# A two-layer decoder trunk on one core: where four table stores are queued, and where the side work stands in the first FFN

## The chip, the cores and the metric

The kernel runs on one core of a Trainium2 chip. The metric is the device time of one execution in microseconds (us). The core has five engines that are fed by queues of their own and run in the order of those queues: TensorE (PE, matmuls), VectorE (DVE), ScalarE (ACT), GpSimd (POOL) and SyncE (SP, which here only issues DMAs).

## The reference

`x` is 512 tokens by 1024 channels, `c` one conditioning vector. All is float32.

```python
c_act = jax.nn.silu(c)
for i in range(2):
    mod = c_act @ w_mod[i] + b_mod[i]
    sh1, sc1, g1, sh2, sc2, g2 = jnp.split(mod, 6, axis=-1)
    h = modulate(rms_norm(x, norm_mix[i]), sh1, sc1)
    y = (stick_breaking_attention, s5_ssm)[i](h, ...)
    x = x + g1[:, None, :] * y
    h = modulate(rms_norm(x, norm_ffn[i]), sh2, sc2)
    x = x + g2[:, None, :] * conv_ffn(h, w_up[i], conv_w[i], conv_b[i], w_down[i])
sh, sc = jnp.split(c_act @ w_fin + b_fin, 2, axis=-1)
return modulate(rms_norm(x, norm_out), sh, sc)

def conv_ffn(h, w_up, conv_w, conv_b, w_down):     # 1024 -> 2 x 2816 -> 1024
    up = causal_depthwise_conv(h @ w_up, width 3) + conv_b
    gate, val = jnp.split(up, 2, axis=-1)
    return (jax.nn.silu(gate) * val) @ w_down
```

The state-space layer `s5_ssm` needs tables that depend on the weights alone: powers of a complex decay, rotation angles, and products of them with its input and output matrices.

## The kernel before, in words

The stages follow each other: attention, first FFN, state-space layer, second FFN with the final norm. The activations lie with channels on the partitions and the 512 tokens along the free dimension. Each float32 matmul is made of three (`mm3`, lines 158, 161 and 162): weights and activations are split into a high part (ACT, line 152) and the rest (DVE, line 153), and high x high, low x high and high x low are summed in PSUM. Every weight tile is 128 x 1024, 512 KB, loaded by SP into one of three raw buffers (line 150) and then split into one of five pairs of buffers.

**First FFN.** The 22 blocks of 128 hidden channels are worked in groups of 8, 8 and 6 (`GROUPS`). A group has an up part, one *unit* per block: 48 matmuls of 128 x 512 for the gate half and the value half, then (`unit_out`) the convolution with three taps (ACT line 441, DVE line 443 twice per half), silu, product (line 453) and the split of the product into gH and gL (lines 457, 458). After the units comes the group's down part (`out_proj`): eight output tiles, each of 24 matmuls in the first two groups, each added to the residual x (line 334). Units 0 and 1 are computed together, ahead of the loop; so the loop starts with the third unit, `up0_2`. In a tile's name the first digit is the layer, the next the unit or group, the last the half or the output tile: `up0_9_1` is the value half of unit 9, `dn0_1_3` the fourth output tile of the second group.

Two kinds of side work are mixed in:

- *Gemvs.* The modulation vectors `mod` of the later layers are 72 products, each of a 128 x 1024 tile of `w_modT` with the broadcast `c_act`: a 512 KB load by SP (line 182, tiles `wg`, two buffers) and one multiply with a sum on DVE (line 183). `bg` (line 201) takes the next one from a list. In the first FFN one follows each output tile of the first two groups, and one follows a unit if the unit's place in its group is below a bound (line 504). The ACT and DVE work of units, weight splits and gemvs is held in program order by `follow`.
- *The preparation* of the state-space tables, `ssm_prep` (lines 828 to 1062), a generator that runs to its next `yield` at each call of `step`. `pace` (line 466) counts microseconds: each unit adds 11.0, each output tile 5.4, and each time 12.0 (`PACE`) are together, one step is taken. Steps 1 to 3 make powers of the decay (`pw`) and the factor `lf`; steps 4 to 8 build rotation tables `tb` in two halves on POOL by doubling (lines 833 to 838, 36 instructions each); step 5 has four transposes of `lf` on PE (line 933, into `ptl`), whose copy `lt` (ACT, line 935) is stored as `sL`. Each half of `tb` is stored by two DMAs to `sR` (line 955); there is one `tb` buffer. Then `b_re` and `b_im` are loaded into `ball` (line 969), POOL makes `bb` of them, and a loop of eight blocks follows, two steps each: POOL makes `bl` from loads `lam` and `bt` (lines 833 to 838) and `cl` from a load `bc` (lines 1036 to 1041), and one step later `direct` (line 976) multiplies `cl` by `bd` in 8 small matmuls on PE (line 980, into `pk0` to `pk7`): four of them need `cl` of line 1038, four that of line 1041. ACT and DVE make `kz` of the result (lines 982, 983), which goes to DRAM.

A scheduler that models time sets the order on each queue; the transposes of line 933 and the matmuls of line 980 are pinned to their place in the program on PE (`pe_pin`). In each queue, what stands behind a waiting instruction waits with it.

Of the kernel before, what the change touches and what calls it, by code (L numbers as in the profile page):

```python
# [41 lines left out]
PACE = 12.0  # L42
# [46 lines left out]
def _trunk(ctx, tc, I, out, tap):  # L89
    nc = tc.nc  # L90
    V, S, G, PE, SP = nc.vector, nc.scalar, nc.gpsimd, nc.tensor, nc.sync
# [13 lines left out]
    def bank(p=None, name="ps"):  # L105
        p = p or mm
        return p.tile([P, 512], F32, tag="b", name=name)
# [84 lines left out]
    def mcol(l, v, j):  # L192
        return l * 48 + v * 8 + j
# [211 lines left out]
    def ffn(l, R, prep=None, last=None, hook=lambda: None):  # L405
        b = mod[:, mcol(l, 3, 0):mcol(l, 3, 0) + KD]
# [3 lines left out]
        with ExitStack() as fc:  # L410
            fp = fc.enter_context(tc.tile_pool(name=f"ffn{l}", bufs=1, reuse_waits="tile"))

            def up_w(i, s):
                return load_w(up_src(l, i, s), name=f"up{l}_{i}_{s}"), bank(name=f"up{l}_{i}_{s}")
# [3 lines left out]
            i0 = 0  # L418
# [41 lines left out]

            i0 = 0
            step = None
            credit = [0.0]


            def pace(us):
# [6 lines left out]
            for gi, gn in enumerate(GROUPS):  # L473
                gs = []
                i = i0
                if gi == 2:
                    hook()
                if gi == 0:
                    if l:
                        hx, ws = pin["hw"]  # L480
                        hd = [(q, s, ws[2 * q + s], bank(name=f"up{l}_{q}_{s}")) for q in range(2) for s in range(2)]
                    else:
                        hx = None
                        hd = [(q, s) + up_w(q, s) for q in range(2) for s in range(2)]
                    head_mm(R, h, a, b, [q[2:] for q in hd])
                    if hx:
                        hx.close()
                    for q in range(4):
                        with behind_head(pin["head"][HEADW[q]]):
                            split_next(False)  # L490
                    pin["prep"] = [pin["split"]]
                    for q in range(2):
                        gs.append(unit_out(q, q, [hd[2 * q + s][3] for s in range(2)]))
                    i = 2
                    step = prep(fc) if prep else (lambda: None)
                for i in range(i, i0 + gn):
                    av = []
                    for s in range(2):
                        w, ps = take(), bank(name=f"up{l}_{i}_{s}")
                        for k in range(KD):  # L500
                            mm3(ps, wk(w, k), (h[0][k], h[1][k]), k == 0, k == KD - 1)
                        av.append(ps)
                    gs.append(unit_out(i, i - i0, av, split_next))
                    if l or i - i0 < (0, 3, 4)[gi]:
                        bg(BGU if l else 1, lined=True)
                    pace(11.0)

                def after():
                    if l == 0 and gi < 2:
                        bg(1, lined=True)  # L510
                    pace(5.4)

                head = None
                if gi == 2 and prep:
                    while step():
                        pass
                    head = [I["w_in"][bi * P:(bi + 1) * P, :] for bi in range(4)], "win"
                R2 = out_proj(lambda mt: I["w_down"][(l * KD + mt) * P:(l * KD + mt + 1) * P, i0 * P:(i0 + gn) * P], gs, mcol(l, 5, 0),
                         acc2 if gi == 2 else None, f"dn{l}_{gi}_", tail=TAIL + (FINT if last else 0), n=gn * P, after=after, last=last if gi == 2 else None, head=head,
                         getw=lambda mt: take(), step=split_next)  # L520
                i0 += gn
# [301 lines left out]
    sR = dram.tile([8, P, 2, 256], F32, tag="sR", name="sR")  # L823
# [4 lines left out]
    def ssm_prep(fc):  # L828
# [14 lines left out]
        def gen():  # L843
# [96 lines left out]
            for hb in range(2):  # L940
                ps_ = slice(hb * HP, (hb + 1) * HP)
                tb = pt_.tile([P, 2, HP, NC], F32, tag="tb", name="tb")
                tt = pt_.tile([P, 2, HP, 32], F32, tag="tt", name="tt")
                E.memset(tb[:, 0, :, 0:1], 1.0)
                E.memset(tb[:, 1, :, 0:1], 0.0)
                for q in range(6):
                    n = 1 << q
                    e0, e1 = bcast(co[:, 3 + q, ps_], n), bcast(si[:, 3 + q, ps_], n)
                    cmul(tb[:, 0, :, n:2 * n], tb[:, 1, :, n:2 * n], tb[:, 0, :, :n], tb[:, 1, :, :n], e0, e1, tt[:, 0, :, :n], tt[:, 1, :, :n])
                    if q > 3:  # L950
                        yield
                    if hb == 0 and q == 4:
                        lf_out()
                for ri in range(2):
                    SP.dma_start(sR[hb * 4:(hb + 1) * 4, :, ri, :].rearrange("b p n -> p b n"), tb[:, ri].rearrange("p (b q) c -> p b (q c)", b=4))
            tc1.close()

            tc2 = ExitStack()
# [342 lines left out]
    b = mod[:, mcol(2, 0, 0):mcol(2, 0, 0) + KD]  # L1301
# [154 lines left out]
```

## Time and profile before

| | |
|---|---|
| runs | 1210.58, 1212.62 and 1214.79 us, median 1212.62 |
| the profiled execution | 1211.41 us, its span (first to last instruction) 1209.4 us |
| PE busy | 1173.0 us, 97% of the span |
| DVE, ACT, POOL busy | 884.2, 563.8 and 264.0 us |
| mean granted TensorE clock | 0.989 of full speed |

A row of a timeline gives the start in us from the span's start, the duration in us, the engine, the line of the kernel, the operation, the tile written, the tiles read and, after x, how many like it were merged; in brackets stands how long the engine sat idle before it and what ended that. Matmuls overlap: the time from one start to the next, not the duration, is what one costs. SPq rows are DMAs being issued, not transferred. A row of a windows table gives the stretch and its length, then the busy time (and count) of PE, weight loads, DVE, ACT and POOL, the granted clock, and the DMA engines' busy share and GB/s.

### The profile page before, as it was taken

The numbers are of one execution on the slowest core, as the hardware profiler recorded it, in microseconds if no ns is written. First come the engines' busy times: TensorE is split into PE (matmuls) and PEld (weight loads), VectorE is DVE, ScalarE is ACT, GpSimd is POOL, SyncE is SP. The second block draws the span as 40 slices with busy tenths as digits, with TensorE's granted clock in tenths as the row PEclk, the third lists the DMA queues.
The fourth block names the chain that finished last, engine by engine and source line by source line (L and its number), as shares of the span: only waits on it lengthen the run. The fifth ranks groups of instructions, "written<-read, shape, count | busy, mean of one in ns | idle before, by whom it ended". The sixth has DMA issues, their size and how long they took to land.

```text
span 1209.4 us, 16352 instructions
## 1 busy us (share of the span) xinstructions
PE 1173.0 (97%) x6182; PEld 962.7 (80%) x6182; DVE 884.2 (73%) x1298; ACT 563.8 (47%) x886; POOL 264.0 (22%) x241
## 2 busy tenths in 40 slices
PE   8999999899999999989999999999999999999997
PEld 6877776588788787868888878789888888888887
DVE  6968888756896399997886679776598457744655
ACT  6756566346553133422444657744554234422443
POOL 1000000000098699989630000000000000000003
PEclk9999999899999999989999999999999999999999
DMA  8875555421234867878665599542257438532221
GB/s 306 319 242 174 192 175 190 157 88 53 73 119 131 239 235 225 252 229 291 217 184 152 188 292 342 186 159 68 70 175 236 130 106 208 157 110 82 79 79 70
DMA packets 93536, 210.99 MB, mean 174 GB/s; under 512 B 19601, under 2 KB 39953, under 8 KB 93458
## 3 DMA queue, kind: packets, MB, share of 16 engines
q1 hardware_dynamic: 85138, 207.86, 54.1%
q10 hardware_dynamic: 8320, 2.10, 0.8%
q8 instruction: 48, 0.79, 0.3%
q14 instruction: 30, 0.25, 0.1%
HBM read 188.68 MB, written 21.24 MB: 174 GB/s over the span
## 4 chain that ended last, share of the span: by engine, by line
PE 66%; DVE 12%; POOL 8%; DMA 6%; ACT 4%; issue 3%; SPq 2%; POOLq 0%; ACTq 0%; DVEq 0%
PE up L161 9%; PE up L162 9%; PE up L158 9%; PE dn L161 5%; PE dn L158 5%; PE dn L162 5%; PE o L756 1%; DMA bt<-in_b_imT_dram 1%; PE wo L158 1%; PE wos L158 1%; DVE ca L443 1%; PE wos L162 1%; PE wos L161 1%; PE wo L162 1%; PE wo L161 1%
## 5 line engine op out<-in xcount | busy, mean ns | idle before, releaser
L162 PE MATMUL up<-hH,up_l 128*128 128x512 f32 (+1 forms) x692 | 265.0, 385 | 4.9 <-DVE up_l L153 4.9
L161 PE MATMUL up<-hL,up_h 128*128 128x512 f32 (+1 forms) x692 | 264.9, 385 | 0.3 <-DVE hL L304 0.2
L158 PE MATMUL up<-hH,up_h 128*128 128x512 f32 (+1 forms) x692 | 261.3, 385 | 1.1 <-ACT hH L298 1.1
L443 DVE SCALAR_TENSOR_TENSOR ca<-up,small,ca 128x511 f32<-128x511 f32 (+1 forms) x176 | 131.4, 747 | 85.4 <-ACT ca L441 82.5
L183 DVE SCALAR_TENSOR_TENSOR wg<-wg,cact 128x1024 f32<-128x1024 f32 x96 | 125.1, 1318 | 42.4 <-DMA wg<-in_w_modT_dram 42.2
L162 PEld LDWEIGHTS up<-hH,up_l 128*128 128x128 f32 x692 | 130.5, 189 | 32.1 <-DVE up_l L153 6.8
L161 PEld LDWEIGHTS up<-hL,up_h 128*128 128x128 f32 x692 | 130.4, 189 | 26.4 <-DVE hL L304 0.9
L158 PEld LDWEIGHTS up<-hH,up_h 128*128 128x128 f32 x692 | 128.3, 188 | 27.9 <-ACT hH L298 1.5
L161 PE MATMUL dn<-gL,dn_h 128*128 128x512 f32 (+1 forms) x394 | 145.5, 369 | 2.7 <-DVE gL L458 2.7
L158 PE MATMUL dn<-gH,dn_h 128*128 128x512 f32 (+1 forms) x394 | 145.7, 371 | 0.5 <-ACT gH L457 0.5
L162 PE MATMUL dn<-gH,dn_l 128*128 128x512 f32 (+1 forms) x394 | 145.3, 369 | 0.0
L152 ACT ACTIVATE up_h<-up_r 128x1024 fp32r<-128x1024 f32 x84 | 88.3, 1053 | 107.6 <-DMA up_r<-in_w_up_dram 54.0
L153 DVE TENSOR_TENSOR up_l<-up_r,up_h 128x1024 fp32r<-128x1024 f32 x84 | 124.5, 1482 | 15.8 <-ACT up_h L152 14.9
L1328 POOL TENSOR_SCALAR xa<-x,Anorm_out 128x256 f32<-128x256 f32 x7 | 5.8, 828 | 576.3 <-ACT dn_h L152 561.5
L441 ACT ACTIVATE ca<-up,small 128x512 f32<-128x512 f32 x88 | 67.8, 771 | 102.4 <-PE up L162 102.4
L161 PEld LDWEIGHTS dn<-gL,dn_h 128*128 128x128 f32 x394 | 74.9, 190 | 15.3 <-DVE gL L458 3.0
L158 PEld LDWEIGHTS dn<-gH,dn_h 128*128 128x128 f32 x394 | 74.8, 190 | 13.7 <-ACT gH L457 0.9
L162 PEld LDWEIGHTS dn<-gH,dn_l 128*128 128x128 f32 x394 | 74.9, 190 | 12.2
L334 DVE SCALAR_TENSOR_TENSOR x<-dn,mod,x 128x512 f32<-128x512 f32 (+1 forms) x55 | 37.3, 679 | 61.1 <-PE dn L162 61.0
L450 ACT ACTIVATE ca<-ca 128x512 f32<-128x512 f32 x44 | 27.8, 633 | 90.1 <-DVE ca L443 88.4
L152 ACT ACTIVATE dn_h<-dn_r 128x1024 fp32r<-128x1024 f32 (+1 forms) x48 | 46.6, 981 | 49.8 <-PE dn L161 36.6
L153 DVE TENSOR_TENSOR dn_l<-dn_r,dn_h 128x1024 fp32r<-128x1024 f32 (+1 forms) x48 | 63.7, 1328 | 3.2 <-ACT dn_h L152 3.0
(304 smaller groups left out, 2258.8 us busy)
## 6 DMA issues: line engine op xcount, KB each, us to landing
wg<-in_w_modT_dram SPq DMA_DIRECT2D x96, 512.0 KB
up_r<-in_w_up_dram SPq DMA_DIRECT2D x84, 512.0 KB
dn_r<-in_w_down_dram SPq DMA_DIRECT2D x32, 512.0 KB
wgs<-in_w_modT_dram SPq DMA_DIRECT2D x16, 512.0 KB
dn_r<-in_w_down_dram SPq DMA_DIRECT2D x16, 384.0 KB
wv_r<-in_w_v_dram SPq DMA_DIRECT2D x8, 512.0 KB
wk_r<-in_w_qk_dram SPq DMA_DIRECT2D x8, 512.0 KB
wq_r<-in_w_qk_dram SPq DMA_DIRECT2D x8, 512.0 KB
```

The lines of the kernel that those rows point to most:

```text
L152: order("S", lambda: S.activation(wh[:, :n], raw[:, :n], AF.Copy))
L153: pin["split"] = order("V", lambda: V.tensor_tensor(wl[:, :n], raw[:, :n], wh[:, :n].bitcast(F32), ALU.subtract))
L158: ins = PE.matmul(ps, ah, bh, start=start, stop=False)
L161: PE.matmul(ps, ah, bl, start=False, stop=False)
L162: PE.matmul(ps, al, bh, start=False, stop=stop)
L183: mul = lambda: V.scalar_tensor_tensor(w, w, 1.0, cact, ALU.mult, ALU.mult, accum_out=raw[:, col:col + 1])
L334: add = lambda: V.scalar_tensor_tensor(xs, pv, gate, xs, ALU.mult, ALU.add)
L441: follow("S", lambda: S.activation(ca, ps, AF.Identity, bias=small[:, cb:cb + 1], scale=tapw[2]))
L443: follow("V", lambda: V.scalar_tensor_tensor(ca[:, q:], ps[:, :T - q], tapw[2 - q], ca[:, q:], ALU.mult, ALU.add))
L450: follow("S", lambda: S.activation(cg, cg, AF.Silu))
L756: ins = PE.matmul(po[pr][h2 * HD:(h2 + 1) * HD, j * P:], vn[:, j, hd:hd + HD], src, start=j == 0, stop=j == 3)
L1328: G.tensor_scalar(xa[k], x[k][:, cb], a[:, k:k + 1], 0.0, ALU.mult, ALU.add)
```

## The change

```diff
             i0 = 0
             step = None
-            credit = [0.0]
+            credit = [PACE]
...
                     gs.append(unit_out(i, i - i0, av, split_next))
-                    if l or i - i0 < (0, 3, 4)[gi]:
+                    if l or i - i0 < (6, 0, 3)[gi]:
                         bg(BGU if l else 1, lined=True)
                     pace(11.0)
...
                 for ri in range(2):
-                    SP.dma_start(sR[hb * 4:(hb + 1) * 4, :, ri, :].rearrange("b p n -> p b n"), tb[:, ri].rearrange("p (b q) c -> p b (q c)", b=4))
+                    G.dma_start(sR[hb * 4:(hb + 1) * 4, :, ri, :].rearrange("b p n -> p b n"), tb[:, ri].rearrange("p (b q) c -> p b (q c)", b=4))
```

The four stores of the rotation tables are issued by POOL instead of SP. Of the seven gemvs that follow units in the first FFN, four now follow units 2 to 5 of the first group (none before), none follow the second group's units (three before), and three follow the third group's (four before); since the list is taken in order, the 16 gemvs in the down parts are the next ones of the list, too. The pace starts with 12.0 to its credit, so each step of the preparation is called one unit, or about two output tiles, earlier; across the border of the first two groups the count falls so that step 11 (with `pk0`) comes two units earlier. The number of instructions of each kind stays.

**The transposes of `lf`.** They are pinned on PE, and now come one unit earlier. PE's queue before, at the end of the first group's up part:

```order
L161 MATMUL up0_7_1_3483<-hL7_2570,up0_7_1_h_3329 128x512
L162 MATMUL up0_7_1_3483<-hH7_2562,up0_7_1_l_3330 128x512
L933 MATMUL ptl_3535<-consts_87,lf_3338 128x128 x4
L158 MATMUL dn0_0_0_3549<-gH0_2887,dn0_0_0_h_3402 128x512
L161 MATMUL dn0_0_0_3549<-gL0_2888,dn0_0_0_h_3402 128x512
L162 MATMUL dn0_0_0_3549<-gH0_2887,dn0_0_0_l_3403 128x512
```

and in the changed kernel:

```order
L161 MATMUL up0_6_1_3419<-hL7_2570,up0_6_1_h_3259 128x512
L162 MATMUL up0_6_1_3419<-hH7_2562,up0_6_1_l_3260 128x512
L933 MATMUL ptl_3471<-consts_87,lf_3271 128x128 x4
L158 MATMUL up0_7_0_3485<-hH0_2555,up0_7_0_h_3335 128x512
L161 MATMUL up0_7_0_3485<-hL0_2563,up0_7_0_h_3335 128x512
L162 MATMUL up0_7_0_3485<-hH0_2555,up0_7_0_l_3336 128x512
```

They moved ahead of unit 7's 48 matmuls. They read `lf`, whose last instruction on POOL is that of line 838. POOL's queue before, around it (`tt` and `tb` are the rotation table's, 16x16 and 512 the two last doublings):

```order
L836 TENSOR_TENSOR lt1_3339<-pw_3063,fi_3066 128x256
L837 TENSOR_TENSOR lt2_3340<-pw_3063,fr_3065 128x256
L835 TENSOR_TENSOR tb_3424<-tt_3425 128x16x16
L838 TENSOR_TENSOR lf_3338<-lt1_3339,lt2_3340 128x8x32
L836 TENSOR_TENSOR tt_3425<-tb_3424,si_3195 128x16x16
L837 TENSOR_TENSOR tt_3425<-tb_3424,co_3194 128x16x16
L838 TENSOR_TENSOR tb_3424<-tt_3425 128x16x16
L833 TENSOR_TENSOR tt_3425<-tb_3424,co_3194 128x512
L834 TENSOR_TENSOR tt_3425<-tb_3424,si_3195 128x512
```

and in the changed kernel, with the first two of the four stores further down:

```order
L838 TENSOR_TENSOR tb_3360<-tt_3361 128x16x16
L836 TENSOR_TENSOR lt1_3272<-pw_2989,fi_2992 128x256
L837 TENSOR_TENSOR lt2_3273<-pw_2989,fr_2991 128x256
L833 TENSOR_TENSOR tt_3361<-tb_3360,co_3124 128x512
L834 TENSOR_TENSOR tt_3361<-tb_3360,si_3125 128x512
L838 TENSOR_TENSOR lf_3271<-lt1_3272,lt2_3273 128x8x32
L835 TENSOR_TENSOR tb_3360<-tt_3361 128x16x32
L836 TENSOR_TENSOR tt_3361<-tb_3360,si_3125 128x512
L837 TENSOR_TENSOR tt_3361<-tb_3360,co_3124 128x512
L955 DMA sR_113<-tb_3360 128x4x256
L838 TENSOR_TENSOR tb_3360<-tt_3361 128x16x32
L955 DMA sR_113<-tb_3360 128x4x256
```

Five instructions of the table that stood behind the last one of `lf` now stand ahead of it, while PE asks for `lf` one unit earlier.

**The first small matmuls, `pk0`.** PE's queue before has them behind unit 10:

```order
L161 MATMUL up0_10_1_4126<-hL7_2570,up0_10_1_h_3994 128x512
L162 MATMUL up0_10_1_4126<-hH7_2562,up0_10_1_l_3995 128x512
L980 MATMUL pk0_4188<-cl_3917,bd_3809 32x128 x8
L158 MATMUL up0_11_0_4216<-hH0_2555,up0_11_0_h_4075 128x512
L161 MATMUL up0_11_0_4216<-hL0_2563,up0_11_0_h_4075 128x512
L162 MATMUL up0_11_0_4216<-hH0_2555,up0_11_0_l_4076 128x512
```

and in the changed kernel behind unit 8, in two halves with three matmuls of unit 9 between:

```order
L161 MATMUL up0_8_1_3978<-hL7_2570,up0_8_1_h_3843 128x512
L162 MATMUL up0_8_1_3978<-hH7_2562,up0_8_1_l_3844 128x512
L980 MATMUL pk0_4037<-cl_3860,bd_3751 32x128 x4
L158 MATMUL up0_9_0_4065<-hH0_2555,up0_9_0_h_3895 128x512
L161 MATMUL up0_9_0_4065<-hL0_2563,up0_9_0_h_3895 128x512
L162 MATMUL up0_9_0_4065<-hH0_2555,up0_9_0_l_3896 128x512
L980 MATMUL pk0_4037<-cl_3860,bd_3751 32x128 x4
L158 MATMUL up0_9_0_4065<-hH1_2556,up0_9_0_h_3895 128x512
L161 MATMUL up0_9_0_4065<-hL1_2564,up0_9_0_h_3895 128x512
```

`pk0` moved two units ahead; `pk1` to `pk7` moved one unit (two output tiles in the down part) ahead.

**SP's queue between the groups.** Before, with what each issue waits for in brackets (DMAHW are earlier DMAs of SP, DMASW those of POOL):

```order
L150 DMA dn0_0_7_r_3716<-in_w_down_dram 128x1024 [waits DMAHW3_49,DVE_49]
L955 DMA sR_113<-tb_3622 128x4x256 [waits DMAHW0_49,Pool_49]
L955 DMA sR_113<-tb_3622 128x4x256 [waits Pool_49]
L182 DMA wg56_3688<-in_w_modT_dram 128x1024 [waits DMAHW2_49,DVE_49]
L150 DMA up0_8_0_r_3757<-in_w_up_dram 128x1024 [waits DMAHW4_49,DVE_49]
L969 DMA ball_3815<-in_b_re_dram 128x512 [waits DMAHW1_49,DMAHW0_49,PE_49]
```

and in the changed kernel:

```order
L150 DMA dn0_0_7_r_3734<-in_w_down_dram 128x1024 [waits DMAHW6_49,DVE_49]
L182 DMA wg60_3706<-in_w_modT_dram 128x1024 [waits DVE_49]
L150 DMA up0_8_0_r_3807<-in_w_up_dram 128x1024 [waits DMAHW7_49,DMAHW3_49,DVE_49]
L182 DMA wg61_3741<-in_w_modT_dram 128x1024 [waits DMAHW4_49,DVE_49]
L150 DMA up0_8_1_r_3842<-in_w_up_dram 128x1024 [waits DMAHW0_49,DVE_49]
L182 DMA wg62_3814<-in_w_modT_dram 128x1024 [waits DVE_49]
L150 DMA up0_9_0_r_3894<-in_w_up_dram 128x1024 [waits DMAHW1_49,DVE_49]
L969 DMA ball_3757<-in_b_re_dram 128x512 [waits DMASW1_49,DMASW2_49,DMASW0_49,DMASW3_49,PE_49,Pool_49]
```

The loads of unit 8's weights and of three gemvs no longer stand behind the stores; the load of `ball`, whose buffer is taken over from the tables, waits on SP for all four stores.

## The prediction

> **What bounds the kernel now.** I read the page's first part, then a table of stretches of 10 us over the first FFN, then the timelines of the engines there.
>
> ```profile
> PE 1173.0 (97%) x6182; PEld 962.7 (80%) x6182; DVE 884.2 (73%) x1298; ACT 563.8 (47%) x886; POOL 264.0 (22%) x241
> ```
>
> PE is the bound, so a change can only take away or add time in which PE waits, or in which its clock is lowered. All edits lie in the first FFN. The table (PE, weight loads, DVE, ACT, POOL, then the granted clock):
>
> ```profile
> 390.00:400.00 10.00, 10.00 (x46) 8.29 (x45) 0.00 (x0) 0.00 (x0) 9.12 (x11) 1.00 0.18 60
> ...
> 410.00:420.00 10.00, 7.78 (x29) 5.97 (x28) 5.32 (x5) 1.06 (x1) 6.83 (x7) 0.85 1.04 284
> ...
> 420.00:430.00 10.00, 10.00 (x44) 8.26 (x44) 10.00 (x11) 3.86 (x4) 9.68 (x7) 0.98 0.64 231
> ...
> 520.00:530.00 10.00, 7.13 (x30) 4.83 (x31) 10.00 (x8) 2.27 (x3) 7.20 (x6) 0.66 0.84 274
> ```
>
> From 390 to 400 us DVE and ACT do nothing at all; PE pays for it afterwards, at 410 to 420 and at 520 to 530, where it is idle and its clock falls. What PE waits for between 270 and 680 us (total, times, longest) and its timeline, with all its waits after 400 us in this FFN:
>
> ```profile
> PE up L162 <- DVE up_l L153: 4.9, 4, 2.2
> PE dn L161 <- DVE gL L458: 2.7, 1, 2.7
> ```
>
> ```profile
> 370.01 0.60 PE L933 MATMUL ptl<-consts,lf 128*128 128x128 f32 x4
> 370.36 0.47 PE L158 MATMUL dn<-gH,dn_h 128*128 128x512 f32 x1
> ...
> 413.99 0.39 PE L158 MATMUL up<-hH,up_h 128*128 128x512 f32 x1
> 414.22 0.39 PE L161 MATMUL up<-hL,up_h 128*128 128x512 f32 x1
> 416.82 0.61 PE L162 MATMUL up<-hH,up_l 128*128 128x512 f32 x1 [2.22 <-DVE up_l L153]
> 417.23 0.63 PE L158 MATMUL up<-hH,up_h 128*128 128x512 f32 x1
> ...
> 428.97 0.39 PE L158 MATMUL up<-hH,up_h 128*128 128x512 f32 x1
> ...
> 450.82 0.64 PE L980 MATMUL pk<-cl,bd 128*32 128x128 f32 x16
> ...
> 463.82 0.50 PE L162 MATMUL up<-hH,up_l 128*128 128x512 f32 x1 [0.79 <-DVE up_l L153]
> ...
> 476.89 0.50 PE L162 MATMUL up<-hH,up_l 128*128 128x512 f32 x1 [1.00 <-DVE up_l L153]
> ...
> 520.20 0.50 PE L158 MATMUL dn<-gH,dn_h 128*128 128x512 f32 x1 [0.46 <-ACT gH L457]
> 523.38 0.80 PE L161 MATMUL dn<-gL,dn_h 128*128 128x512 f32 x1 [2.67 <-DVE gL L458]
> ```
>
> The down part from 370.36 to 413.99 holds 192 matmuls, 0.227 us each; a unit of 48 takes 10.91. Unit 8 runs from 413.99 to 428.97, 14.98 us: 4.1 more than that, 2.4 of it the wait at 416.82 and 1.7 the half clock behind it (0.41 from 416.82 to 417.23). The four later waits sum to 4.9 idle, some 0.2 more each for restarting (0.50 instead of 0.39), and the clock of 0.66 means 6.8 us at half, of which some 3.2 fall on matmuls: 8.9 in all. The fourth wait of the first row, 0.89 at 327 us, lies ahead of all edits but a gemv and stays. So **13.0 us** is what the FFN could gain. The cause stands on SP and DVE:
>
> ```profile
> 374.44 4.85 SPq L150 DMA_DIRECT2D dn_r<-in_w_down_dram  x2
> 395.36 3.87 SPq L955 DMA_DIRECT2D sR<-tb  x2
> ...
> 402.81 0.33 SPq L969 DMA_DIRECT2D ball<-in_b_re_dram  x1
> ```
>
> ```profile
> 404.30 1.22 DVE L183 SCALAR_TENSOR_TENSOR wg<-wg,cact 128x1024 f32<-128x1024 f32 x1 [15.96 <-DMA wg<-in_w_modT_dram]
> ...
> 414.50 2.27 DVE L153 TENSOR_TENSOR up_l<-up_r,up_h 128x1024 fp32r<-128x1024 f32 x1
> ...
> 473.16 1.52 DVE L443 SCALAR_TENSOR_TENSOR ca<-up,small,ca 128x511 f32<-128x511 f32 x2
> ...
> 512.84 1.52 DVE L443 SCALAR_TENSOR_TENSOR ca<-up,small,ca 128x511 f32<-128x511 f32 x2
> ```
>
> SP issues nothing between 379.3 and 395.4: the second table's stores wait for POOL, and the loads of gemvs and of unit 8's weights stand behind them. DVE idles 15.96 us for a gemv's load, splits unit 8's weights late (414.50), and is behind PE until 523.
>
> **The stores and the loads that they held.** Off SP's queue, the stores no longer hold `wg` and `up0_8`; unit 8 starts without the wait: **-4.1**. SP now waits at `ball` instead, with `wg63` and `up0_9_1` behind. That is late by some 10 us for DVE, but `up0_9_1` is needed only when PE has done the first half of unit 9, after 440 (below). I cost it at nothing; with that cover gone it would be up to 6.
>
> **The gemvs.** One costs DVE 1.22 (row at 404.30) to, with POOL busy, 2.27 as the split of the same size. Four more in units 2 to 5 are 4.9 to 9.1 of DVE work, which delay splits; whatever PE loses by that before `pk0` is hidden by its wait there. In the second group, units without gemvs start their convolution at 473.16 (unit 11) and 512.84 (unit 15): 9.9 us each on DVE against 10.91 on PE. So once DVE is not behind, it stays so, and the later waits go: **-8.9**. In the third group PE never waits in this trace; one gemv less there is worth nothing.
>
> **The preparation.** Here PE starts to wait for POOL. POOL's timeline before:
>
> ```profile
> 357.49 0.74 POOL L838 TENSOR_TENSOR lf<-lt,lt 128x256 f32<-128x256 f32 x1
> 358.19 0.63 POOL L836 TENSOR_TENSOR tt<-tb,si 128x256 f32<-128x256 f32 x1
> ...
> 363.87 2.15 POOL L835 TENSOR_TENSOR tb<-tt 128x512 f32<-128x512 f32 x1
> ...
> 368.57 2.14 POOL L838 TENSOR_TENSOR tb<-tt 128x512 f32<-128x512 f32 x1
> 374.54 0.13 POOL L944 MEMSET tb<- 128x16 f32 x1 [3.83 <-DMA sR<-tb]
> ...
> 387.72 0.62 POOL L833 TENSOR_TENSOR tt<-tb,co 128x256 f32<-128x256 f32 x1
> ...
> 397.55 1.28 POOL L838 TENSOR_TENSOR tb<-tt 128x512 f32<-128x512 f32 x1
> ...
> 406.32 1.26 POOL L833 TENSOR_TENSOR t<-ball,fr 128x512 f32<-128x512 f32 x1 [6.80 <-DMA ball<-in_b_re_dram]
> ...
> 418.23 1.27 POOL L834 TENSOR_TENSOR t<-lam,bt 128x512 f32<-128x512 f32 x1 [2.54 <-DMA bt<-in_b_imT_dram]
> ...
> 435.11 2.29 POOL L1038 TENSOR_TENSOR cl<-t,t 128x576 f32<-128x576 f32 x1
> ...
> 440.41 1.43 POOL L1041 TENSOR_TENSOR cl<-t,t 128x576 f32<-128x576 f32 x1
> ...
> 462.69 2.37 POOL L1041 TENSOR_TENSOR cl<-t,t 128x576 f32<-128x576 f32 x1
> ```
>
> *Transposes.* PE gets there one unit earlier, at 370.01 - 10.91 = 359.1. The five table instructions now ahead of `lf`'s last took 358.19 to 363.87, 5.7; so `lf` is ready at 357.49 + 0.74 + 5.7 = 363.9. PE waits 4.8. A wait of 2.22 cost one stretch of half clock worth 1.7, the pair around 523 some 3.2; I take 2.5: **+7.3**. What else moves with the step waits too, and is covered: ACT's copy `lt` holds unit 6's silu, whose result PE needs only in the down part, after 376; the store `sL` on SP holds `dn0_0_3`, which DVE splits behind unit 7's work, after 376 as well. Unit 8 then ends at 413.99 + 10.91 + 7.3 = 432.2.
>
> *`pk0`* needs `cl`, which in this trace is ready at 440.41 + 1.43 = 441.84, 9 us before PE asks (450.82). Now PE asks at 432.2. When is `cl` ready? The first table still ends at 370.7. Issuing a store is not seen on POOL in this trace: between nothing (SP's issue of two took 3.87 with its waits) and one DVE instruction in the way (2.27) each; nearest is a small one, 0.5, with two ahead of the second table and two behind: +1 and +1. Landing as before, 3.83, or up to 4.5 more. The second table starts at 375.5. It took 374.54 to 398.83, 24.3, but DVE was idle under its last twelve instructions (387.72 to 398.83, 11.1); a 128x512 one took 1.28 there and 2.15 at 363.87 with DVE at work. Between +0 and +5, I take +2: done at 401.8, stores issued by 402.8. From there to the first use of `ball` it is 7.5, as before (398.83 to 406.32): 410.3. From `ball` to `cl` it took 35.5 (406.32 to 441.84). The waits for `bt` (3.0 with a small one ahead of it) should go, since no weights are queued in between: 32.5, to 36.5 if DVE is in the way. So `cl` is ready at **442.8**, bounds 438.8 (370.7 + 3.8 + 24.3 + 7.5 + 32.5) and some 456.
>
> PE waits for the first half of `cl` (4.4 earlier, as 437.40 to 441.84), does three matmuls, and waits on: the fourth matmul of unit 9 starts at 443.1, in this trace at 428.97 + 0.7 = 429.7, with 0.35 for `pk0` still to come there. That is 13.1 behind; 2.5 for the clock, as above, makes **+15.6**, in which the 4.1 and the 7.3 are contained. Behind `pk0` wait `kz` on ACT and DVE (lines 982, 983), with unit 8's gH and gL and the split of `up0_10_1` queued behind them; PE needs that split one and a half units after `pk0`, so I cost it at nothing. Later `pk`s find POOL ahead: a block takes POOL 23.2 us (441.84 to 465.06), while unit for unit PE needs 32 to reach `pk1` and 22 for each of the next.
>
> **Sum:** +15.6 - 8.9 = +6.7. Every us of `cl` beyond 432.2 is one us of PE. Against the profiled execution (1209.4 of span and 2.0 around it, 1211.41) this is 1218.1; the median of the runs is 1.2 above that execution, so I put the median at **1219**. Bounds of `cl` give 1215 to 1232.
>
> One page speaks against these stores: the Trainium skill, "SBUF — State Buffer", section "SBUF: two separate sides", says that a DMA issued by GpSimd can sit until VectorE leaves the port that the two share, since GpSimd must write the descriptors. The trace shows the sharing (1.28 against 2.15 for the same POOL instruction), but no store of POOL. That page of the Trainium skill ties the blocking to VectorE's two-port modes; if it held for the instructions here, rival C below would be the forecast.
>
> **Rivals.**
>
> *A: POOL is in time (faster).* If `cl` is ready by 432.2, PE does not wait at `pk0`, and only the transposes cost: +7.3 - 4.1 - 8.9 = -5.7, 1207. It decides at the point where `cl` comes at 436.1 (sum zero). For it: PE's wait at the transposes leaves DVE less to do, and DVE's work is what stretches POOL. Against it: POOL would need to gain 10 us, while DVE, no longer stopped by SP, now works beside the second table. If `lf` were in time too, 1200. Chance 0.16.
>
> *B: both in balance.* `cl` between 432.7 and 439.7: within 0.3% of 1212.6, about what a measurement of this kernel can tell from no change. Chance 0.18.
>
> *C: the stores hold POOL.* If each of the four waits for a DVE instruction of 2.27 instead of 0.5, `cl` comes 7 later: 1226. It is not more likely, since nothing in this trace shows such a wait. Chance 0.12.
>
> *D: the hold on SP only moves.* `ball` waits for the stores; were `up0_9_1` late, the 8.9 would stay in part, 1219 to 1227. Its cover is PE's wait at `pk0`; contained in the forecast's upper side.
>
> The forecast has 0.54, the largest, because POOL's path to `cl` is long and hardly shorter than before, while PE's request comes 18 us earlier. Faster by over 0.3% is A, 0.16; within 0.3% is B, 0.18; slower is the forecast with C, 0.66. The range holds A's 1207 and C's 1226: 1206.5 to 1227.5, with some 0.06 left out below and 0.1 above.
>
> **What would show it.** In the changed profile: SP issuing through 380 to 395 and DVE busy there; no wait of PE at unit 8's start; a wait of 4 to 6 us at the transposes and one of some 10, in two pieces, at `pk0`, each with a lowered clock behind it; POOL's `cl` (line 1041) ending at 439 to 448; no waits of PE near 463, 477 and 520. The forecast is wrong if POOL ends `cl` by 436, or if PE waits for splits in the second group though no gemvs stand there.

## The result, and the profile after

| | before | after |
|---|---|---|
| median of the runs, us | 1212.95 (4 runs, 1210.58 to 1214.79) | 1223.00 (4 runs, 1220.05 to 1224.71) |
| ratio, 95% interval | | 1.0093 [1.0073, 1.0113] |
| profiled execution, span, us | 1211.41, 1209.4 | 1223.06, 1221.0 |
| first FFN in the trace, us | 387.08 | 393.67 |

The change makes the kernel slower, by 10 us of median or 0.93%. The first FFN is taken from its first matmul to the first of the state-space layer. Both stand behind a wait of 1.15 that no kernel here changes. These are their rows before, then after:

```profile
285.67 0.74 PE L158 MATMUL up<-hH,up_h 128*128 128x256 f32 x4 [1.15 <-ACT hH L298]
...
672.75 0.74 PE L158 MATMUL u<-hH,win_h 128*128 128x256 f32 x4 [1.15 <-ACT hH L298]
```

```profile
290.45 0.74 PE L158 MATMUL up<-hH,up_h 128*128 128x256 f32 x4 [1.15 <-ACT hH L298]
...
684.12 0.73 PE L158 MATMUL u<-hH,win_h 128*128 128x256 f32 x4 [1.15 <-ACT hH L298]
```

The difference of the two executions is thus 6.6 in the FFN (393.67 - 387.08), 4.8 ahead of it (290.45 - 285.67), where no edit is, and 0.2 behind it. The part ahead is taken up near the end.

The table of stretches of the changed kernel, columns as in the prediction's:

```profile
390.00:400.00 10.00, 10.00 (x46) 8.29 (x45) 6.19 (x7) 2.01 (x2) 9.37 (x12) 1.00 0.50 152
400.00:410.00 10.00, 10.00 (x46) 8.29 (x45) 10.00 (x11) 2.13 (x2) 9.84 (x6) 1.00 0.79 260
410.00:420.00 10.00, 10.00 (x46) 8.29 (x45) 4.23 (x6) 2.12 (x2) 5.03 (x7) 1.00 0.62 196
420.00:430.00 10.00, 10.00 (x45) 8.28 (x45) 4.14 (x5) 1.06 (x1) 9.64 (x9) 1.00 0.89 314
...
440.00:450.00 10.00, 4.39 (x23) 2.52 (x24) 2.65 (x6) 1.05 (x3) 9.69 (x8) 0.66 0.87 250
...
520.00:530.00 10.00, 10.00 (x58) 7.93 (x57) 9.27 (x8) 4.71 (x7) 8.21 (x6) 1.00 0.55 175
```

DVE works again in 390 to 410, and PE is whole at 410 to 420 and at 520 to 530, where it had waited before. In their place stands 440 to 450: PE busy for 4.39 of 10 us at a mean clock of 0.66, with POOL busy nearly throughout (9.69). What PE waits for in the FFN (total, times, longest), and the rows of its timeline:

```profile
PE ptl L933 <- POOL lf L838: 7.0, 1, 7.0
PE pk L980 <- POOL cl L1038: 5.1, 1, 5.1
...
PE pk L980 <- POOL cl L1041: 1.7, 1, 1.7
```

```profile
371.32 0.69 PE L933 MATMUL ptl<-consts,lf 128*128 128x128 f32 x2 [7.04 <-POOL lf L838]
371.66 0.78 PE L158 MATMUL up<-hH,up_h 128*128 128x512 f32 x1
...
375.37 0.40 PE L158 MATMUL up<-hH,up_h 128*128 128x512 f32 x1
...
443.89 0.65 PE L980 MATMUL pk<-cl,bd 128*32 128x128 f32 x8 [5.09 <-POOL cl L1038]
...
447.84 0.65 PE L980 MATMUL pk<-cl,bd 128*32 128x128 f32 x8 [1.72 <-POOL cl L1041]
448.42 0.80 PE L158 MATMUL up<-hH,up_h 128*128 128x512 f32 x1
...
453.63 0.39 PE L158 MATMUL up<-hH,up_h 128*128 128x512 f32 x1
```

Every wait of PE that the change added is for POOL, at the two pinned places. The wait of 0.89 ahead of the edits is still there; the others of the kernel before are gone. POOL's rows that set them, and what SP and DVE did meanwhile:

```profile
369.57 1.70 POOL L838 TENSOR_TENSOR lf<-lt,lt 128x256 f32<-128x256 f32 x1
...
374.57 0.93 POOL L955 DMA_DIRECT2D sR<-tb  x1
...
377.15 0.77 POOL L955 DMA_DIRECT2D sR<-tb  x1 [0.31 <-POOL tb L838]
380.89 0.12 POOL L944 MEMSET tb<- 128x16 f32 x1 [2.97 <-DMA sR<-tb]
...
399.15 2.02 POOL L833 TENSOR_TENSOR tt<-tb,co 128x512 f32<-128x512 f32 x1
...
409.32 0.80 POOL L955 DMA_DIRECT2D sR<-tb  x1
...
411.90 0.77 POOL L955 DMA_DIRECT2D sR<-tb  x1 [0.30 <-POOL tb L838]
418.08 1.05 POOL L833 TENSOR_TENSOR t<-ball,fr 128x512 f32<-128x512 f32 x1 [4.65 <-DMA ball<-in_b_re_dram]
...
446.39 1.40 POOL L1041 TENSOR_TENSOR cl<-t,t 128x576 f32<-128x576 f32 x1
```

```profile
406.50 0.33 SPq L150 DMA_DIRECT2D up_r<-in_w_up_dram  x1
415.41 0.33 SPq L969 DMA_DIRECT2D ball<-in_b_re_dram  x1
```

```profile
425.83 1.68 DVE L183 SCALAR_TENSOR_TENSOR wg<-wg,cact 128x1024 f32<-128x1024 f32 x1 [7.99 <-DMA wg<-in_w_modT_dram]
```

SP is held again, from 406.5 to 415.4, now at `ball`, and DVE idles 7.99 for the gemv behind it. In this kernel that costs nothing that the trace shows: PE stands at `pk0` until 447.8, and behind that it waits for no split.

### The profile page after: what moved, and what is told of

Read it like the earlier page. It is cut to its first block, busy times and chain, and to the rows that moved or that the text cites. A ratio compares the mean times of both kernels' runs of the same rounds, so it can differ in the third digit from the quotient of the medians.

```text
span 1221.0 us, 16357 instructions
## 1 busy us (share of the span) xinstructions
PE 1176.5 (96%) x6182; PEld 966.4 (79%) x6182; DVE 872.3 (71%) x1298; ACT 564.9 (46%) x886; POOL 263.7 (22%) x245
## 4 chain that ended last, share of the span: by engine, by line
PE 75%; POOL 8%; DVE 7%; DMA 4%; ACT 3%; issue 2%; SPq 0%; POOLq 0%; ACTq 0%; DVEq 0%
PE up L161 11%; PE up L158 11%; PE up L162 11%; PE dn L158 5%; PE dn L162 5%; PE dn L161 5%; PE o L756 1%; PE wo L158 1%; PE wos L158 1%; PE wo L162 1%; PE wos L162 1%; PE wos L161 1%; PE wo L161 1%; DVE om L726 1%; PE v L158 1%
## 5 line engine op out<-in xcount | busy, mean ns | idle before, releaser
L162 PEld LDWEIGHTS up<-hH,up_l 128*128 128x128 f32 x692 | 131.1, 190 | 27.3 <-DVE up_l L153 1.3
L161 PEld LDWEIGHTS up<-hL,up_h 128*128 128x128 f32 x692 | 131.2, 190 | 26.3 <-DVE hL L304 0.9
L183 DVE SCALAR_TENSOR_TENSOR wg<-wg,cact 128x1024 f32<-128x1024 f32 x96 | 122.4, 1289 | 30.7 <-DMA wg<-in_w_modT_dram 30.3
L153 DVE TENSOR_TENSOR up_l<-up_r,up_h 128x1024 fp32r<-128x1024 f32 x84 | 121.7, 1449 | 10.5 <-ACT up_h L152 9.5
```

The lines of the kernel that those rows point to most:

```text
L153: pin["split"] = order("V", lambda: V.tensor_tensor(wl[:, :n], raw[:, :n], wh[:, :n].bitcast(F32), ALU.subtract))
L161: PE.matmul(ps, ah, bl, start=False, stop=False)
L162: PE.matmul(ps, al, bh, start=False, stop=stop)
L183: mul = lambda: V.scalar_tensor_tensor(w, w, 1.0, cact, ALU.mult, ALU.mult, accum_out=raw[:, col:col + 1])
```

## The experiments

All times are medians; the ratio is to the kernel before on the same chip. FFN is read in each trace as above, so it is one execution's, which can lie some us off the median: the profiled executions of e1, e4 and e11 took 1208.05, 1204.04 and 1208.43.

| kernel | median, us (runs) | ratio, 95% interval | FFN, us | PE's wait at the transposes, at `pk0` |
|---|---|---|---|---|
| before | | | 387.08 | 0, 0 |
| after | 1223.00 (4) | 1.0093 [1.0073, 1.0113] | 393.67 | 7.0, 5.1 + 1.7 |
| e1 stores + gemvs | 1212.71 (12) | 1.0010 [0.9994, 1.0026] | 383.77 | 0, 0 |
| e2 pace | 1219.50 (6) | 1.0060 [1.0043, 1.0076] | 390.68 | 0, 10.5 + 3.3 |
| e3 stores | 1213.34 (12) | 1.0016 [1.0003, 1.0030] | 385.48 | 0, 0 |
| e4 gemvs | 1208.65 (12) | 0.9968 [0.9953, 0.9983] | 377.21 | 0, 0 |
| e5 stores + pace | 1220.02 (6) | 1.0074 [1.0058, 1.0091] | 391.76 | 0, 12.8 + 3.3 |
| e6 gemvs + pace | 1221.46 (5) | 1.0090 [1.0071, 1.0108] | 394.84 | 7.1, 6.5 + 3.3 |
| e7 after, transposes later | 1223.29 (5) | 1.0102 [1.0082, 1.0123] | 394.47 | 0, 16.0 + 1.7 |
| e8 after, short table | 1210.14 (12) | 0.9991 [0.9980, 1.0003] | 383.44 | 7.0, 0 |
| e9 e1, loads on POOL | 1214.45 (12) | 1.0024 [1.0008, 1.0039] | 388.31 | 0, 2.0 + 3.5 |
| e10 e9, `pk0` later | 1211.50 (12) | 0.9990 [0.9976, 1.0004] | 383.29 | 0, 0 |
| e11 after, `pk0` later | 1211.42 (12) | 0.9995 [0.9986, 1.0004] | 383.82 | 7.05, 0 |

**The theory**: the pace sends PE to two pinned places before POOL is ready, and that alone costs. The rivals: the stores on POOL cost it, or the gemvs in the first group do.

### e1: the change without its pace

```diff
-            credit = [PACE]
+            credit = [0.0]
```

> The changed kernel with the credit back at 0, so only the stores and the gemvs are changed. Theory (PE waits for POOL at two pinned places, the transposes and pk0, because the pace asks for them earlier): the transposes stand behind unit 7 again and PE asks for lf 11 us later than in the changed kernel, where it waited 7.0 for it, so no wait there; pk0 stands behind unit 10, asked for at about 446.7 (450.8 less the 4.1 of unit 8's start), and cl is ready near 442 (second table stretched from 24.3 to some 30.7, then 29.7 from ball to cl as in the changed kernel), so no wait there either. What is left is the whole gain of 13: 1200 us (1197 to 1204), under both kernels. Rival 'the four stores on POOL cost the time': 1210 or more, as they are in this kernel too. Rival 'the gemvs in the first group cost the time by stretching POOL': also above 1206, with a wait of PE for POOL somewhere.

Measured: 1212.71, no gain. No wait at the two places, as the theory has it; but the gain of 13 is missing, and that part of it falls. The time alone lies in the range of both rivals, so it does not decide between them and the theory; e2, e5 and e6 do. SP's queue (what it waited for between 385 and 415, in all, times, longest), DVE and PE show where it went:

```profile
SPq L969 <- DMA sR<-tb: 22.1, 2, 19.7
```

```profile
421.36 1.79 DVE L183 SCALAR_TENSOR_TENSOR wg<-wg,cact 128x1024 f32<-128x1024 f32 x1 [17.68 <-DMA wg<-in_w_modT_dram]
```

```profile
455.47 0.50 PE L158 MATMUL up<-hH,up_h 128*128 128x512 f32 x1 [2.13 <-ACT up_h L152]
...
521.22 0.50 PE L161 MATMUL dn<-gL,dn_h 128*128 128x512 f32 x1 [2.66 <-DVE gL L458]
```

SP stands at `ball` for the second table as it had stood at the stores in the kernel before (its waits there between 375 and 400):

```profile
SPq L955 <- POOL tb L835: 16.0, 1, 16.0
SPq L955 <- POOL tb L838: 3.1, 1, 3.1
```

DVE has its hole again (17.68, before 15.96), and PE pays at 455 and at 521. The hold only moved. e9 and e10 test that.

### e2: the pace alone

```diff
-            credit = [0.0]
+            credit = [PACE]
```

(to the kernel before)

> The kernel before with the credit at PACE, stores on SP and gemvs as before. Theory: PE waits at the transposes (4 to 7 us, lf not ready) and at pk0, which stands behind unit 8; the second table runs beside an idle DVE as before (24.3 us), cl is ready near 442, the fourth matmul of unit 9 starts near 442 instead of 429.7, and the later waits, 8.9 in all, go since PE is late by more than DVE. Sum +12 + 2.5 for the clock - 8.9: 1219 us (1214 to 1223), about as slow as the changed kernel although neither stores nor gemvs are changed. Rival 'the stores cost the time': within 3 us of the kernel before.

Measured: 1219.50, ratio 1.0060 [1.0043, 1.0076], as expected, and the rival on the stores falls: they are on SP here. What PE waits for:

```profile
PE pk L980 <- POOL cl L1038: 10.5, 1, 10.5
...
PE pk L980 <- POOL cl L1041: 3.3, 1, 3.3
```

The later waits of the kernel before (463 to 523) are gone here too, though stores and gemvs are as they were. That PE's stand of 13.8 at `pk0` gives DVE the time is the likely reason; it was not tried by itself. The wait of 2.22 at unit 8's start is gone as well, and it lies ahead of `pk0`: the split that PE waited for there ends 128.8 us after the FFN's start (416.71 + 2.07 - 289.98), in the kernel before at 131.1 (414.50 + 2.27 - 285.67). The wait at the transposes that was expected (4 to 7) is not there; e5 says why.

### e3 and e4: the stores alone, the gemvs alone

```diff
-                    SP.dma_start(sR[hb * 4:(hb + 1) * 4, :, ri, :].rearrange("b p n -> p b n"), tb[:, ri].rearrange("p (b q) c -> p b (q c)", b=4))
+                    G.dma_start(sR[hb * 4:(hb + 1) * 4, :, ri, :].rearrange("b p n -> p b n"), tb[:, ri].rearrange("p (b q) c -> p b (q c)", b=4))
```

(e3)

```diff
-                    if l or i - i0 < (0, 3, 4)[gi]:
+                    if l or i - i0 < (6, 0, 3)[gi]:
```

(e4)

> The kernel before with the four stores on POOL alone. Theory: SP issues on through 380 to 395, unit 8 starts without its wait of 2.2 (-4.1), DVE has no hole of 16 us and so little backlog in the second group; the three gemvs there (1.2 to 2.3 of DVE each beside 9.9 of 10.9) may keep one or two of the small waits. PE does not wait for POOL. 1200 to 1206 us, forecast 1202. Rival 'the stores cost the time': 1215 or more, with a POOL store that holds POOL for 2 us or more or a later cl that PE waits for.

> The kernel before with the gemvs moved alone. Theory: SP is still held by the stores of the second table, so unit 8's wait stays (4.1), but in the second group DVE has 1.2 to 2.3 less per unit in three units and catches up, so part of the later 8.9 goes: 1204 to 1211 us, forecast 1207. The four gemvs in the first group stretch lf by 1 to 3 us, which the transposes behind unit 7 do not see (PE asks 11.8 after lf was ready). Rival 'the gemvs cost the time': 1216 or more.

Measured: e3 1213.34, a little slower than before and 11 above the forecast; e4 1208.65, faster, near its forecast. In e3 PE waits 5.1 for splits in the up parts (0.9 of it ahead of the edits) and 4.4 at the second down part: again the hold at `ball` (DVE's longest wait for a gemv's load is 15.6). In e4 the stores still hold SP and DVE idles 16.6. Yet the wait at unit 8's start, which was expected to stay, is gone: the gemv ahead of its split waits 0.85 for its load instead of 5.33, and the split ends 128.0 us after the FFN's start (413.77 + 2.30 - 288.05), not 131.1. In the second group no gemvs stand, and DVE makes most of the loss good. Of PE's waits behind unit 8 in this FFN these are left:

```profile
435.61 0.50 PE L162 MATMUL up<-hH,up_l 128*128 128x512 f32 x1 [0.69 <-DVE up_l L153]
...
519.13 0.50 PE L161 MATMUL dn<-gL,dn_h 128*128 128x512 f32 x1 [0.69 <-DVE gL L458]
```

Of the three edits the gemvs alone bring something, 0.32% [0.17, 0.47], the fastest version found. In its profiled execution the FFN is 9.9 shorter, but that is the lowest of its 12 runs; 3.9 us is what the medians give.

### e5 and e6: the change without the gemvs, without the stores

```diff
-                    if l or i - i0 < (6, 0, 3)[gi]:
+                    if l or i - i0 < (0, 3, 4)[gi]:
```

(e5, in the changed kernel)

```diff
-                    G.dma_start(sR[hb * 4:(hb + 1) * 4, :, ri, :].rearrange("b p n -> p b n"), tb[:, ri].rearrange("p (b q) c -> p b (q c)", b=4))
+                    SP.dma_start(sR[hb * 4:(hb + 1) * 4, :, ri, :].rearrange("b p n -> p b n"), tb[:, ri].rearrange("p (b q) c -> p b (q c)", b=4))
```

(e6, in the changed kernel)

> The changed kernel with the gemvs as before (stores on POOL and pace changed). Theory: the time is set by when POOL is ready at the transposes and at pk0. Without the four gemvs in units 2 to 5 DVE stretches POOL less ahead of lf (in the changed kernel lf came 34.1 us after co, 25.9 before), so the first wait is 3 to 6 instead of 7.0, but the wait at pk0 grows by as much, since cl hardly moves: 1217 to 1222 us, forecast 1220; one or two small waits in the second group may stay behind pk0. Rival 'the gemvs in the first group cost it': 1213 or less.

> The changed kernel with the four stores back on SP (gemvs and pace changed). Theory: the wait at the transposes stays near 7, SP is held until the second table is done, DVE is idle under its last instructions and so the table is shorter (24 to 26 instead of 30.7); ball is loaded right behind; cl comes at or some us ahead of the changed kernel's, and PE waits for it at pk0 as there: 1214 to 1222 us, forecast 1218. Rival 'the stores on POOL cost it': 1212 or less, with no wait at pk0.

Measured: 1220.02 and 1221.46; neither edit is the cause of the loss. The wait at the transposes is 7.1 in e6 and 0 in e5: it comes with the gemvs, not with the pace alone. In e5 POOL's last instruction of `lf` ends 72.6 us after the FFN's start (361.48 + 0.75 - 289.66), in the changed kernel 80.8 (369.57 + 1.70 - 290.45):

```profile
361.48 0.75 POOL L838 TENSOR_TENSOR lf<-lt,lt 128x256 f32<-128x256 f32 x1
```

That is 8.2 later. Most of it is the order: the five instructions of the table that stand ahead of `lf`'s last in the changed kernel stand behind it in e5, and in the changed kernel's trace they take 6.3 (359.79 to 361.94, 362.64 to 363.78 and 366.58 to 369.57); some 1.9 are left for longer instructions. The order comes with the gemvs. In the four traces without that edit (before, e2, e3, e5) `lf` ends 72.5 to 72.6 us after the FFN's start, in the nine with it 79.5 to 80.8, also where it is the only edit (e4, 365.81 + 1.72 - 288.05 = 79.5):

```profile
365.81 1.72 POOL L838 TENSOR_TENSOR lf<-lt,lt 128x256 f32<-128x256 f32 x1
```

So the wait needs both edits: the gemvs make `lf` late, and the pace makes PE ask early. Without the gemvs the wait at `pk0` is longer instead, 16.1 against 6.8.

### e7: the transposes where they were

```diff
-                    if hb == 0 and q == 4:
+                    if hb == 0 and q == 5:
                         lf_out()
```

> The changed kernel with lf_out called one step later, so that the transposes stand behind unit 7, where they were before; pk0 stays behind unit 8. Theory: the first wait (7.0) goes, but PE then comes to pk0 some 10 us earlier and waits that much longer for the same cl: the end of pk0 hardly moves, 1219 to 1224 us, forecast 1221, with a wait at pk0 of 15 us or so in place of 7.0 and 6.8. Rival 'two waits that add': 1212 to 1215, 7.0 and the half clock behind it off.

Measured: 1223.29, no better than the changed kernel. 7.0 of wait are taken away at the transposes, and 10.9 come back at `pk0` (16.0 + 1.7 against 5.1 + 1.7): the rival 'two waits that add' falls. Of the two, `cl` alone decides the time.

### e8: a shorter second table

```diff
-                    cmul(tb[:, 0, :, n:2 * n], tb[:, 1, :, n:2 * n], tb[:, 0, :, :n], tb[:, 1, :, :n], e0, e1, tt[:, 0, :, :n], tt[:, 1, :, :n])
+                    if hb == 1 and q > 3:
+                        E.memset(tb[:, :, :, n:2 * n], 0.0)
+                    else:
+                        cmul(tb[:, 0, :, n:2 * n], tb[:, 1, :, n:2 * n], tb[:, 0, :, :n], tb[:, 1, :, :n], e0, e1, tt[:, 0, :, :n], tt[:, 1, :, :n])
```

> The changed kernel without the last two doublings of the second half of the rotation tables (24 instructions become 2 memsets, so columns 16 to 63 of that half are zero): work on POOL is left out. Theory: those instructions took some 18 us in the changed kernel; without them cl is ready some 15 us earlier, ahead of PE's arrival at pk0 (5.1 + 1.7 of waits and 10.2 us of half clock there), so PE waits only at the transposes: 1209 to 1214 us, forecast 1212. Rival 'POOL does not set the time': no change, 1221 to 1224.

Measured: 1210.14. `cl` ends 145.4 us after the FFN's start (431.52 + 1.44 - 287.57; the edit moves its line to 1044) instead of 157.3, and PE does not wait for it. By the ratios (0.9991 for 1.0093) 12 us go:

```profile
431.52 1.44 POOL L1044 TENSOR_TENSOR cl<-t,t 128x576 f32<-128x576 f32 x1
```

Of PE's waits for POOL one is left:

```profile
PE ptl L933 <- POOL lf L838: 7.0, 1, 7.0
```

### e9 and e10: the loads behind the table on POOL's queue as well

e9 is e1 with the following but for the last two added lines; the loads of `lam` and `bt` (`load_bl`) get the same argument as that of `bc`. e10 is e9 with the two lines.

```diff
-                SP.dma_start(ball[:, ri].rearrange("p a b -> p (a b)"), I[("b_re", "b_im")[ri]])
+                G.dma_start(ball[:, ri].rearrange("p a b -> p (a b)"), I[("b_re", "b_im")[ri]])
...
-            def held(out, in_):
-                tc.keep_in_program_order(SP.dma_start(out, in_))
+            def held(out, in_, e=SP):
+                tc.keep_in_program_order(e.dma_start(out, in_))
...
-                    held(bc[:, ri].rearrange("p a b -> p (a b)"), I[("c_re", "c_im")[ri]][:, bi * 64:(bi + 1) * 64])
+                    held(bc[:, ri].rearrange("p a b -> p (a b)"), I[("c_re", "c_im")[ri]][:, bi * 64:(bi + 1) * 64], SP if bi else G)
...
+                if bi == 1:
+                    yield
                 if owe:
                     direct(*owe)
```

> e1 (stores and gemvs changed, pace as before) with the eight loads that take over the tables' buffers (ball, and lam, bt and bc of the first block) on POOL's queue too, so that nothing of SP waits for the second table. In e1 SP issued nothing from 390.1 to 412.4, DVE sat idle 17.7 for a gemv's load, and PE waited 2.13 and 0.53 near 455 and 2.66 near 521. Theory now (the change does not free SP, it moves the hold from the stores to ball): that hole of DVE goes, and the three waits with it. POOL pays for eight more issues at some 0.8 and for loads that are issued later, so cl comes 5 to 8 later than e1's 447.2, and PE, which asked at 447.0 in e1, waits 4 to 8 at pk0: 1209 to 1214 us in all, forecast 1211. Rival 'the waits of e1 do not come from the hold': DVE's hole goes, and PE still waits near 455 and 521 in the same places, with pk0's wait on top: 1216 or more.

> As e9, with one more yield ahead of the first call of direct, so that pk0 stands behind unit 11 and PE comes to it 11 us later. Theory (hold moved, and POOL late only where PE is sent to it early): no hole of DVE, no wait at pk0, and so nearly none of the waits of the kernel before: 1203 to 1207 us, forecast 1205, at or a little under the kernel with the gemvs alone (1208.65). Rival 'something else of the stores costs 4 us against the gemvs alone': 1209 to 1213.

Measured: 1214.45 and 1211.50, both above the range expected. In both DVE's hole is gone (its longest wait for a gemv's load is 1.9 and 2.8), and so is the wait near 455: these came from the hold. The wait at the second down part stays in e9 (2.7 and 1.6) and is gone in e10, so the hold is not shown to be its cause. In e9 PE waits 2.0 + 3.5 at `pk0` instead of near 455. In e10 it does not, yet a new wait stands at 476.80, at the start of unit 13. SP's queue between 420 and 452, and PE:

```profile
SPq L988 <- POOL bl L838: 22.5, 1, 22.5
```

```profile
476.80 0.50 PE L158 MATMUL up<-hH,up_h 128*128 128x512 f32 x1 [4.01 <-ACT up_h L152]
```

The next DMA on SP that POOL feeds, the store of the first block's `bl` (`sB`), now holds it for 22.5. Unit 12's first weights are issued behind it, at 454.27, and unit 13's behind the next block's `sB`, at 469.19; for these PE waits. The hold moved once more, to the next place where SP's queue meets POOL's work. That the rival's 'something else' (1209 to 1213, where e10 lies) is this hold is read from the trace and was not tried by a run.

### e11: `pk0` where it was

```diff
+                if bi == 1:
+                    yield
                 if owe:
                     direct(*owe)
```

(in the changed kernel; `pk0` stands behind unit 10 again, `pk1` behind unit 12)

> The changed kernel with one more yield ahead of the first call of direct: pk0 to pk7 stand where they stood in the kernel before (pk0 behind unit 10), the transposes stay one unit early. Theory (what costs is that PE is sent to pk0 before POOL has cl): the waits of 5.1 and 1.7 at pk0 and the half clock there go; the 7.0 at the transposes stays with its half clock: 1208 to 1213 us, forecast 1210, as in e8, with POOL's work all done. Rival 'PE has to wait for POOL's total anyway': a wait appears at pk0 behind unit 10 or at a later pk, and the time stays at 1218 or more.

Measured: 1211.42, ratio 0.9995 [0.9986, 1.0004]. POOL does all its work, and with `pk0` and the later `pk`s alone moved back 11.6 us of the changed kernel's median are gone. PE's only wait for POOL is here:

```profile
366.65 0.69 PE L933 MATMUL ptl<-consts,lf 128*128 128x128 f32 x2 [7.05 <-POOL lf L838]
```

Together with e8 this settles the cause: PE is sent to `pk0` two units early, and POOL's `cl` is not ready. The 7.05 at the transposes, which is left in e11, is no loss against e1 (1212.71), which has no wait there and pays at 455 and 521 instead. From the second half of `pk0` to the end of the FFN the five kernels that wait there behind unit 8 take nearly the same, 236.3 in the changed one (684.12 - 447.84), 236.3 in e2, 235.7 in e5, 236.5 in e6 and 235.2 in e7.

## Why the prediction was right, and where its steps were not

The direction, the mechanism (PE waits for POOL at the two pinned places) and the place were right; 1219 was forecast, 1223.00 measured. That the sum for the FFN comes out within 0.1 us is in part luck, as its terms show. By its steps, in us from the FFN's start where the two executions are compared (so 4.8 is taken off the changed one's times):

- **The transposes.** PE there at 359.1 forecast, 359.3 measured (363.9 + 0.2 for the first pair, less 4.8); `lf` at 363.9 forecast, 366.5 measured, so the wait is 7.04, not 4.8. The half clock behind it cost 1.7 (9 matmuls from 371.66 to 375.37, 3.71 instead of 2.04), not 2.5. Together 8.7 against 7.3. The five instructions ahead of `lf`'s last were costed nearly rightly (5.7, measured 6.3; the other 2.0 are longer instructions ahead of them and `lf`'s own). That the gemvs put them there it did not see, and the expectation for e2 put the wait down to the pace alone (7.0 in the four kernels with both edits and the transposes early, none in e2 and e5).
- **`cl`** at 442.8 forecast, 443.0 measured (446.39 + 1.40 - 4.8). It is met by errors that cancel. The second table took 30.7 (380.89 to 411.59) instead of 26.3, with DVE at work under its last instructions (2.02 for a 128x512 instruction at 399.15, 1.05 at 418.08 beside an idle DVE), and POOL's issues took 0.77 to 0.93 instead of 0.5. On the other side the landing took 2.97 instead of 3.83, the last store to the first use of `ball` 5.4 (412.67 to 418.08) instead of 7.5, and `ball` to `cl` 29.7 (418.08 to 447.79) instead of 32.5.
- **`pk0`.** The fourth matmul of unit 9 was to be 13.1 behind; it is 13.9 (448.42 - 290.45 against 429.7 - 285.67). The half clock behind it cost 2.5, as taken (12 matmuls from 448.42 to 453.63, 5.21 instead of 2.72).
- **The later waits**: 8.9 forecast; 9.8 is what the other terms leave (13.9 + 2.5 - 6.6), not a reading of its own. The 0.2 that the prediction takes for each restart is 0.11 by the rows it cites (0.50 instead of 0.39). **Sum**: +6.7 forecast, +6.6 in the FFN of the trace.

The step that failed is "Off SP's queue, the stores no longer hold `wg` and `up0_8`; unit 8 starts without the wait", with the **13.0 us** that "the FFN could gain" resting on it. The loads do come early (in e1 SP issues them up to 390.1, and unit 8 starts without its wait), but nothing is gained: without the pace, stores and gemvs together bring 0.10% [-0.06, 0.26] of loss (e1), since SP then stands for 22.1 at `ball`, and for 22.5 at `sB` when `ball` is off its queue (e10). The prediction named `ball` and costed it at nothing "with that cover", PE's wait at `pk0`, and at up to 6 without; in this kernel the cover was there, so the sum held. Nor are the two gains those of the edits that they were put down to. Unit 8's wait (the -4.1) also goes with the pace alone (e2) and with the gemvs alone (e4), the stores on SP in both. The -8.9 was put down to gemvs and DVE, while in e2 the pace alone takes those waits away. The gemvs' other step, "whatever PE loses by that before `pk0` is hidden by its wait there", is nearly right: 0.19% of the 0.93 (e5 against after, with intervals that overlap), by a `cl` that comes 1.3 later in the trace (447.84 - 290.45 against 445.75 - 289.66).

Rival C does not occur: four issues of 0.77 to 0.93 on POOL, none of 2.27, and `cl` is not late by them. By the Trainium skill, "SBUF — State Buffer", section "SBUF: two separate sides", GpSimd cannot write its descriptors while VectorE runs an instruction in a two-port mode; these stores show no such wait, and whether VectorE ran such an instruction beside them the trace does not say. The same section says of the shared port that the engine which starts first keeps it for its whole instruction. The trace shows that one form of POOL instruction takes 2.02 beside a busy DVE and 1.05 beside an idle one, which fits; which engine kept the port it does not show.

**What stays open.** The 4.8 us ahead of the FFN. In the 13 traces the FFN starts between 285.3 and 290.5; before's, at 285.67, is 3.0 under their median of 288.7, the changed kernel's the latest. 2.5 us of the 4.8 arise in the first 21 us: the 16 `stat` matmuls take 1.93 us before and 3.55 after. Those 2.5 do not go with the wait at `pk0`: the row of 3.55 also stands in e3, e8 and e10, which do not wait there, and e6, which does, has 1.93. But the five kernels in which PE waits at `pk0` behind unit 8 also have the five latest starts (289.2 to 290.5), though `pk0` lies 150 us further on; whether that is chance was not tried. In the medians the whole 10 us go when `pk0` is moved back (e11) or `cl` comes earlier (e8); the traces show how 6.6 of them arise, and how the rest does is open. The two rows of the `stat` matmuls, before and after:

```profile
12.02 1.93 PE L251 MATMUL stat<-ones,sq 128*128 128x1 f32 x16
```

```profile
13.01 3.55 PE L251 MATMUL stat<-ones,sq 128*128 128x1 f32 x16
```

## What to carry to other kernels

A pinned matmul that reads side work moves the wait of the slow engine onto PE: before moving it earlier, compare when its input is ready with when PE will ask, as `cl` here: ready at 443, asked for at 434 (443.89 - 5.09 - 4.8). A queue that is held by one engine's results is not freed by moving one DMA off it: the next DMA in it that needs those results holds it instead (19.1 us at the stores, 22.1 at `ball`, 22.5 at `sB`), so look down the queue to the end. Two waits on one chain need not add: taking the first away (e7) gave nothing, taking the last away (e11) gave the whole loss back. And an edit can act through the scheduler far from its own line: moving the gemvs put five POOL instructions ahead of `lf`.

## What the runs showed of the hardware

- TensorE's granted clock fell to half around waits of PE, in the kernel before behind one of 2.22 and one of 2.67, each shorter than the stretch of half clock that followed. The rows of stretches (the third number from the end is the clock) for these two, then for the changed kernel around the end of the wait of 7.04 and of those of 5.09 and 1.72:

```profile
417.10:420.40 3.30, 3.30 (x9) 2.51 (x9) 1.28 (x2) 0.09 (x1) 2.13 (x3) 0.50 1.03 369
523.00:529.60 6.60, 6.22 (x28) 4.29 (x29) 6.60 (x7) 1.06 (x1) 3.94 (x3) 0.50 0.89 267
```

```profile
368.30:374.90 6.60, 3.58 (x10) 2.90 (x11) 3.35 (x5) 2.73 (x4) 6.52 (x7) 0.50 0.41 120
443.40:453.40 10.00, 7.79 (x31) 5.15 (x32) 4.53 (x4) 0.91 (x2) 9.69 (x8) 0.50 0.80 219
```

  The first stretch is some 3.4 us long (0.85 and 0.98 in the two stretches of 10 us around it, in the prediction's table), the second 6.8 (0.66 in 520 to 530), the last at least 10.0. The one of the third row begins by 368.3, while PE still waits until 371.32, so only its rest falls on matmuls. What a wait cost beyond itself is 1.7 and 2.5 in the changed kernel, and 1.7 and some 3.2 in the kernel before by the prediction's reading. The Trainium skill, "TensorE: Matmul & The Clock Gate", section "Part 1: The HAM clock gate (the "warmup" mystery)", puts the fall behind one idle window of about 3.4 us; the stretches agree with that window's length, the waits of 2.22 and 2.67 that sufficed do not.
- A DMA issue took POOL 0.77 to 0.93 us of its time for the tables' stores in the changed kernel and 0.55 to 0.62 for the loads in e9, against 0.33 for a weight load on SP (row at 406.50).
